# Every TensorE operand on a multiple of 512 bytes: padded and reordered buffers in a one-core decoder layer

## The chip, the cores and the metric

One core of a Trainium2 chip runs the whole kernel. The metric is device microseconds, from three runs. TensorE is called PE in the profile (PEld is its weight load), VectorE DVE, ScalarE ACT, GpSimd POOL and SyncE SP. On-chip memory has 128 partitions; an address here is the byte within a partition.

## The reference

One layer of a decoder over 512 tokens and 1024 channels, float32. The heart of it is matmuls: an input projection of 1024 to 8968 columns that feeds four token mixers (sliding-window attention A, a conformer convolution B, forgetting attention C, block-sparse attention D) and their gates; a projection of each branch back to 1024; the output projection; and a gated feed-forward part of 1024 to 5632 and 2816 to 1024.

```python
h = rmsnorm(x, ln1_g)
z = h @ w_in
(qa, ka, va, ub, qc, kc, vc, fc, qd, kd, vd, gz) = jnp.split(z, IN_SPLITS, axis=-1)
gates = jax.nn.sigmoid(gz.reshape(bsz, seq, N_BRANCH, D_MODEL) + b_gate)
ya = sliding_window_gqa(qa, ka, va, sinks, rel_bias[:, :SWA_HEADS])
yb = conformer_conv(ub, conv_w, conv_b, conv_ln_g, conv_ln_b)
yc = forgetting_attention(qc, kc, vc, fc, b_fgate)
yd = moba_attention(qd, kd, vd, rel_bias[:, SWA_HEADS:])
branches = jnp.stack([ya, yb, yc, yd], axis=2)
proj = jnp.einsum('bsnc,ncd->bsnd', branches, w_br)
merged = jnp.einsum('bsnd,bsnd->bsd', gates, proj)
x = x + merged @ w_out
h2 = rmsnorm(x, ln2_g)
u = causal_depthwise_conv(h2 @ w_up, ffn_conv_w, ffn_conv_b)
g_ff, v_ff = jnp.split(u, 2, axis=-1)
x = x + (jax.nn.silu(g_ff) * v_ff) @ w_down
return rmsnorm(x, final_g)
```

## The kernel before

Each float32 operand is split into a high and a low part, both of type float32r, and a product is made of three matmuls: high by high, low by high, high by low. The activations of the first norm are `hh` and `hl`, `[128, 8, 512]` each: eight slices of 128 channels by 512 tokens, 2048 bytes a slice. Weights come from HBM into `raw` (two buffers), ACT copies a half of a slab into `whi`, DVE subtracts to get `wlo` (three buffers each, taken in turn), and PE reads both. A dense unit is one block of 128 output channels: for k = 0 to 7 a trio, `whi` by `hh`, `wlo` by `hh`, `whi` by `hl`, 24 matmuls of 512 columns, with the 128x128 weight tile as the stationary operand and a slice of `hh` or `hl` as the moving one (line 244, in `t_mm`). V projections (line 297) have it the other way round: slices of `hh` stationary, weights moving, 256 or 264 columns. So have the output projection (lines 971 and 1013: slices of `merged` stationary, weights moving) and the down projection (line 1122: slices of `ah` and `al` stationary). Attention (lines 454, 455, 482, 509 and their like for branch A) reads `stA`, `stD`, `stE`, `stG`, `P`, `PTh`, `PTl` and `v`. In the feed-forward part `hh` and `hl` are used again for the second norm's output; the down projection's resident weights `wdh`, `wdl` take the same place afterwards.

Order is written out: a list of units, each followed by pieces of attention heads, evictions, splits and loads at fixed steps. Every tile comes from a pool with a stack on one side of the memory. `P0` (left, from the bottom) lives through the kernel; above it come `PI` (first norm), then `P1` (attention), then `PX` and `PW` (output projection). On the right side, from the top downwards, stand `PR` (one pad), `PY` (`acc` and the eight `y` buffers), later `PF` (`ah`, `al` and the feed-forward tiles). Tiles of a pool follow one another in the order of their first allocation; a ring of buffers takes the size of its largest tile, so `whi` and `wlo` take 4224 bytes, those of the first slab's `[128, 4, 264]` halves. Below `P0` lie 16384 bytes for the descriptors of GpSimd's transfers, then 128 bytes of constants.

GpSimd issues 18 transfers right after the first V units (lines 1336 to 1351: mask, bias rows, tables), later small ones of one row each for branch C (line 379). The bias rows in `rows` are transposed on PE at line 1361, `rb32` (the bias table) is a stationary operand at line 1374. The convolution's filters run on DVE between.

Of the kernel before, what the change touches and what calls it, by code (L numbers as in the profile page):

```python
# [8 lines left out]
F32 = mybir.dt.float32  # L9
R32 = mybir.dt.float32r  # L10
# [20 lines left out]
BR_A, BR_B, BR_C, BR_D = 0, 1, 2, 3  # L31
GL = 640
C_ID, C_TRI, C_MASK, C_N = 0, 128, 640, 1152


def f(ap):
    return ap.bitcast(F32)
# [16 lines left out]
def hybrid_layer_kernel(ctx: ExitStack, tc: tile.TileContext, x, ln1_g, w_in, b_gate, b_fgate, sinks,  # L54
                        conv_w, conv_b, conv_ln_g, conv_ln_b, w_br, w_out, ln2_g, w_up, ffn_conv_w,
                        ffn_conv_b, w_down, rel_bias, final_g, cst, onehot, gmask, out):
    nc = tc.nc
# [4 lines left out]
    def dap(t, off, ap):  # L62
        return bass.AP(tensor=t.tensor, offset=t.offset + off, ap=[list(a) for a in ap])

    def pool(name, side=None, space=None, bufs=1):
        kw = dict(name=name, bufs=bufs, reuse_waits="tile")
        if side:
            kw["side"] = side
        if space is not None:
            kw["space"] = space  # L70
        if space == DRAM:
            kw.pop("reuse_waits")
        return tc.alloc_tile_pool(**kw)

    P0 = pool("p0")
# [4 lines left out]
        return PD.tile([128, 512], F32, name="dps", tag="dps", bufs=3)  # L80


    ident = P0.tile([128, 128], F32, name="ident")
    hh = P0.tile([128, KD, S], R32, name="hh", tag="hh")
    hl = P0.tile([128, KD, S], R32, name="hl", tag="hl")
    pcA = P0.tile([128, 92], F32, name="pcA")
    pcB = P0.tile([128, 124], F32, name="pcB")
    pcC = P0.tile([128, 128], F32, name="pcC")
    nsk = P0.tile([128, 8], F32, name="nsk")
    sk = P0.tile([128, 8], F32, name="sk")  # L90
    bfg = P0.tile([128, 8], F32, name="bfg")
    P0.tile([128, 8], F32, name="pad")

    def col_gate(n, j):
        return pcA[:, n * 8 + j:n * 8 + j + 1]
# [45 lines left out]
        SP.dma_start(xs[t], dap(x, t * 128 * D, [[D, 128], [1, D]]))  # L141


    NRAW, NSP = 2, 3
    raws = []
    halves = []

# [13 lines left out]
    class Half:  # L161
# [10 lines left out]
        def split(self):  # L172
            src = self.raw.t[:, self.ks, self.cs]
            if self.dst is None:
                shape = [128, self.ks.stop - self.ks.start, self.cs.stop - self.cs.start]
                self.hi = P0.tile(shape, R32, name="whi", tag="whi", bufs=NSP)
                self.lo = P0.tile(shape, R32, name="wlo", tag="wlo", bufs=NSP)
            else:
                self.hi, self.lo = self.dst()
            yield ACT.activation(self.hi, src, AF.Copy)  # L180
            yield DVE.tensor_tensor(self.lo, src, f(self.hi), op=OP.subtract)  # L181
            self.raw.left -= 1
# [82 lines left out]


    PR = pool("pr", side="right")
    PR.tile([128, 8], F32, name="pad")
    PY = pool("py", side="right")
    acc = PY.tile([128, KD, S], F32, name="acc")  # L270

# [673 lines left out]
    def wo_load():  # L945
        PX = ctxP["px"] = pool("px")
        for t in range(NT):
            xt = PX.tile([128, D], F32, name="x1_%d" % t)
            SP.dma_start(xt, dap(x, t * 128 * D, [[D, 128], [1, D]]))
            x1.append(xt)  # L950
        PW = ctxP["pw"] = pool("pw")
        WO["h"] = PW.tile([128, KD, 512], R32, name="woh")
        WO["l"] = PW.tile([128, KD, 512], R32, name="wol")
        n2["g"] = PW.tile([128, D], F32, name="g2")
        SP.dma_start(n2["g"], dap(ln2_g, 0, [[0, 128], [1, D]]))
        n2["ss"] = PX.tile([128, 2, NT], F32, name="ss2")
        PX.tile([128, 8], F32, name="pad")

    oa = []

# [76 lines left out]
    def ffn_open():  # L1037

        PF = ctxP["pf"] = pool("pf", side="right")
        ffn["ah"] = PF.tile([128, NF, S], R32, name="ah")  # L1040
        ffn["al"] = PF.tile([128, NF, S], R32, name="al")
        n2["rb"] = PF.tile([128, S], F32, name="rb")
        ffn["fg"] = None

# [281 lines left out]
    PI.release()  # L1326
    PIP.release()
    P1 = ctxP["p1"] = pool("p1")
    rows = P1.tile([128, 3, 128], F32, name="rows", tag="P", bufs=2)
    em = P1.tile([32, 2 * GL], F32, name="em", tag="PTh", bufs=1)  # L1330
    gs = P1.tile([16, GL], F32, name="gs", tag="PTl", bufs=1)
    rb32 = P1.tile([32, 16], F32, name="rb32")
    Gd = PDR.tile([16, GL], F32, name="Gd")
    Gw = PDR.tile([128, 16, GL], F32, name="Gw")
    tm = ctxP["p1"].tile([128, 1024], F32, name="tm", tag="va", bufs=1)
# [61 lines left out]
    for u in units:  # L1397
# [4 lines left out]
        if u.adv:  # L1402
            step += 1
            if step == REL:
                ctxP["p1"].release()
                ctxP["ps1"].release()
                ctxP["w"] = pool("ps2", space=PSUM)
                wo_load()
            ps_ = head_pieces(step) + pieces.get(step, [])
# [12 lines left out]
        if u.idx == UP0:  # L1422
            u.out = u.mm(n2_last, 2)
            PY.release()
            ctxP["pw"].release()
            ffn_open()
            n2_rstd_dve()
        elif u.idx == UP0 + 1:
            u.out = u.mm(n2_rstd_pe, 4)
        elif u.idx >= NT:  # L1430
            u.out = u.mm()
# [73 lines left out]
```

## Time and profile before

| | |
|---|---|
| median of 3 runs | 1012.38 us (1012.28 to 1012.4) |
| profiled execution | 1012.8 us, its span 1011.0 us |
| instructions | 12462, of which 4840 matmuls |
| granted TensorE clock | 0.999 |
| HBM read, written | 99.10 MB, 7.51 MB |

The span is the time from the first to the last instruction that the trace shows; the execution's own time holds what lies around it. A row of a timeline has the start, the duration, the engine, the line, the operation, and the tiles as out<-in. Matmuls are pipelined: a duration of about 400 ns is the way of one matmul through the array, and the next one starts well before it ends. The distance from start to start is the rate at which PE goes on.

### The profile page before, as it was taken

Reading aid. Unit: us, or ns where it says so; the run is one execution under the profiler, and the core shown is the slowest. Engines: PE = TensorE matmul, PEld = TensorE weight load, DVE = VectorE, ACT = ScalarE, POOL = GpSimd, SP = SyncE. Lnnn points to the kernel's source line nnn. Section 1 sums busy time; section 2 is a strip of 40 time slices with the busy share of each in tenths; the row PEclk is TensorE's granted clock in tenths of the full one; section 3 lists DMA queues with packets and bytes.
Section 4 is the critical chain, followed back from the end, with each engine's and each line's share of the span. In section 5 each row is a group of like instructions: output and inputs, shape, how many; then the busy total and the mean of one; then the engine's idle time right before and its main releaser. Section 6 shows DMA issues by size and latency. Waiting matters only on the chain.

```text
span 1011.0 us, 12462 instructions
## 1 busy us (share of the span) xinstructions
PE 999.1 (99%) x4840; PEld 826.8 (82%) x4840; DVE 666.9 (66%) x1188; ACT 448.4 (44%) x782; POOL 23.2 (2%) x49
## 2 busy tenths in 40 slices
PE   8999999999999999999999999999999999999997
PEld 6888887989888888888888888888888888888886
DVE  6557777777878688896665445677767677733404
ACT  5435455455455545557424233443444444432302
POOL 1300000000000000000000000000000000000000
PEclk9999999999999999999999999999999999999999
DMA  7435532132233133232136430232233223334102
GB/s 251 105 112 186 164 85 85 42 105 81 67 107 122 43 84 100 66 97 93 42 125 208 146 125 1 84 125 84 83 100 109 84 84 110 120 124 146 63 1 84
DMA packets 101099, 102.18 MB, mean 101 GB/s; under 512 B 3377, under 2 KB 88544, under 8 KB 101040
## 3 DMA queue, kind: packets, MB, share of 16 engines
q1 hardware_dynamic: 99264, 99.31, 31.0%
q0 software_dynamic: 1200, 1.03, 0.4%
q10 hardware_dynamic: 576, 1.05, 0.3%
q8 instruction: 38, 0.62, 0.3%
q14 instruction: 21, 0.17, 0.1%
HBM read 99.10 MB, written 7.51 MB: 105 GB/s over the span
## 4 chain that ended last, share of the span: by engine, by line
PE 92%; DVE 4%; ACT 2%; issue 1%; DMA 1%; SPq 0%; DVEq 0%; ACTq 0%
PE dps L244 63%; PE wps L1122 8%; PE dps L1122 5%; PE dps L297 4%; PE dps L1013 2%; PE wps L971 2%; PE tps L482 2%; PE yps L509 1%; PE sps L455 1%; PE sps L454 1%; ACT P L437 1%; DMA raw<-in_w_in_dram 1%; PE yps L627 1%; DVE stE L386 1%; DVE P L475 1%
## 5 line engine op out<-in xcount | busy, mean ns | idle before, releaser
L244 PE MATMUL dps<-hh,whi 128*128 128x512 f32 x848 | 337.5, 398 | 0.0
L244 PE MATMUL dps<-hh,wlo 128*128 128x512 f32 x848 | 336.0, 396 | 0.0
L244 PE MATMUL dps<-hl,whi 128*128 128x512 f32 x848 | 332.0, 392 | 0.0
L181 DVE TENSOR_TENSOR wlo<-raw,whi 128x1024 fp32r<-128x1024 f32 (+1 forms) x152 | 185.5, 1222 | 95.2 <-ACT whi L180 95.0
L180 ACT ACTIVATE whi<-raw 128x1024 fp32r<-128x1024 f32 (+1 forms) x152 | 159.6, 1054 | 97.9 <-PE wps L1122 37.9
L244 PEld LDWEIGHTS dps<-hl,whi 128*128 128x128 f32 x848 | 161.2, 190 | 37.5
L244 PEld LDWEIGHTS dps<-hh,whi 128*128 128x128 f32 x848 | 159.5, 188 | 35.7 <-ACT v L307 0.2
L244 PEld LDWEIGHTS dps<-hh,wlo 128*128 128x128 f32 x848 | 159.4, 188 | 33.4
L437 ACT ACTIVATE P<-P,nm 128x128 f32<-128x128 f32 (+2 forms) x96 | 50.9, 531 | 76.9 <-DVE nm L435 76.3
L244 PE MATMUL dps<-y,whi 128*128 128x512 f32 x256 | 83.8, 399 | 0.0
L710 DVE SCALAR_TENSOR_TENSOR co<-hc,pcB,co 128x489 f32<-128x489 f32 (+25 forms) x120 | 82.5, 730 | 0.4
L1086 DVE SCALAR_TENSOR_TENSOR uy<-u,pcC,uy 128x511 f32<-128x511 f32 x88 | 65.8, 747 | 1.5
L244 PEld LDWEIGHTS dps<-y,whi 128*128 128x128 f32 x256 | 48.2, 188 | 10.9
L1078 DVE TENSOR_TENSOR u<-dps,rb 128x512 f32<-128x512 f32 x44 | 30.2, 687 | 36.8 <-PE dps L244 34.1
L244 PE MATMUL dps<-y,wlo 128*128 128x512 f32 x128 | 50.4, 394 | 0.0
L495 ACT ACTIVATE PTh<-tps 128x512 fp32r<-128x512 f32 (+1 forms) x48 | 24.4, 525 | 42.3 <-PE tps L482 41.9
L1122 PE MATMUL wps<-wlo,ah 128*128 128x512 f32 (+1 forms) x116 | 42.7, 368 | 0.0
L1122 PE MATMUL wps<-whi,ah 128*128 128x512 f32 (+1 forms) x116 | 42.7, 368 | 0.0
L1122 PE MATMUL wps<-whi,al 128*128 128x512 f32 (+1 forms) x116 | 42.7, 368 | 0.0
L1100 ACT ACTIVATE ah<-uy 128x512 fp32r<-128x512 f32 x22 | 13.9, 632 | 60.3 <-DVE uy L1099 60.3
L539 ACT ACTIVATE ytmp<-yps 64x512 f32<-64x512 f32 x24 | 14.3, 594 | 48.1 <-PE yps L509 24.9
L1092 ACT ACTIVATE uy<-uy 128x512 f32<-128x512 f32 x22 | 13.9, 632 | 43.6 <-DVE uy L1086 43.6
(250 smaller groups left out, 1292.7 us busy)
## 6 DMA issues: line engine op xcount, KB each, us to landing
raw<-in_w_up_dram SPq DMA_DIRECT2D x22, 1024.0 KB, 5.1
raw<-in_w_in_dram SPq DMA_DIRECT2D x40, 512.0 KB, 3.9
raw<-in_w_in_dram SPq DMA_DIRECT2D x14, 1024.0 KB, 5.2
raw<-in_w_down_dram SPq DMA_DIRECT2D x10, 1024.0 KB, 5.1
raw<-in_w_br_dram SPq DMA_DIRECT2D x16, 512.0 KB, 3.5
Gw<-Gd SPq DMA_DIRECT2D x8, 640.0 KB, 7.0
x<-in_x_dram SPq DMA_DIRECT2D x8, 512.0 KB, 8.5
raw<-in_w_out_dram SPq DMA_DIRECT2D x4, 1024.0 KB, 5.1
```

Of the source, the lines that this page charges most:

```text
L180: yield ACT.activation(self.hi, src, AF.Copy)
L181: yield DVE.tensor_tensor(self.lo, src, f(self.hi), op=OP.subtract)
L244: PE.matmul(ps, lhsT=a, rhs=b, start=n == 0, stop=n == 3 * nk - 1)
L297: PE.matmul(ps[:, :n], lhsT=l, rhs=r[:, k % 4, :], start=not done, stop=len(done) == 3 * KD - 1)
L437: ACT.activation(P[:, sl], P[:, sl], AF.Exp, bias=nm[:, i:i + 1], scale=-1.0, accum_out=sm[:, i:i + 1])
L482: PE.transpose(ps[:, c:c + 128], o["P"][:, PO[qb] + kb * 128:PO[qb] + kb * 128 + 128], ident)
L495: ACT.activation(o["PT"][0][:, sl], ps[:, :c], AF.Copy)
L710: DVE.scalar_tensor_tensor(co[c][:, d:], hc[:, :S - d], col_cw(CW - 1 - d, c), co[c][:, d:], op0=OP.mult, op1=OP.add)
L971: PE.matmul(oa[t], lhsT=l, rhs=r, start=k == 0 and i == 0, stop=k == KD - 1 and i == 2)
L1078: DVE.tensor_tensor(u, ps, n2["rb"], op=OP.mult)
L1086: DVE.scalar_tensor_tensor(y[:, d:], u[:, :S - d], col_fw(2 - d, j), y[:, d:], op0=OP.mult, op1=OP.add)
L1122: PE.matmul(ps, lhsT=l, rhs=r, start=k == first_k and i == 0, stop=k == last_k and i == 2)
```

## The change

No instruction is added, removed or put elsewhere; only the places of tiles differ.

- A tile `lead` of 384 bytes comes first in `P0`, and the area for GpSimd's descriptors shrinks from 16384 to 8192 bytes.
- The rings `whi` and `wlo` are allocated right behind `hh` and `hl`, each buffer 1152 floats (4608 bytes); a half takes the first part of it.
- The pads at the ends of `P0`, `PR`, `PX` grow, and `PF` gets one behind `al`.
- `rb32` is no tile of its own but a fourth slice of `rows`.

```diff
+LEAD, PADS, WPAD = 96, (136, 120, 88, 56), 1152
...
+    lead = P0.tile([128, LEAD], F32, name="lead")
     ident = P0.tile([128, 128], F32, name="ident")
     hh = P0.tile([128, KD, S], R32, name="hh", tag="hh")
     hl = P0.tile([128, KD, S], R32, name="hl", tag="hl")
+    NRAW, NSP = 2, 3
+    for n in ("whi", "wlo"):
+        for _ in range(NSP):
+            P0.tile([128, WPAD], R32, name=n, tag=n, bufs=NSP)
...
-    P0.tile([128, 8], F32, name="pad")
+    P0.tile([128, PADS[0]], F32, name="pad")
...
-                self.hi = P0.tile(shape, R32, name="whi", tag="whi", bufs=NSP)
-                self.lo = P0.tile(shape, R32, name="wlo", tag="wlo", bufs=NSP)
+                self.hi, self.lo = (P0.tile([128, WPAD], R32, name=n, tag=n, bufs=NSP)[:, :shape[1] * shape[2]].rearrange(
+                    "p (k c) -> p k c", k=shape[1]) for n in ("whi", "wlo"))
...
-    PR.tile([128, 8], F32, name="pad")
+    PR.tile([128, PADS[1]], F32, name="pad")
...
-        PX.tile([128, 8], F32, name="pad")
+        PX.tile([128, PADS[2]], F32, name="pad")
...
         ffn["al"] = PF.tile([128, NF, S], R32, name="al")
+        PF.tile([128, PADS[3]], F32, name="pad")
...
-    rows = P1.tile([128, 3, 128], F32, name="rows", tag="P", bufs=2)
+    rows = P1.tile([128, 4, 128], F32, name="rows", tag="P", bufs=2)
...
-    rb32 = P1.tile([32, 16], F32, name="rb32")
+    rb32 = rows[:32, 3, :16]
...
-    nc = bacc.Bacc("TRN2", target_bir_lowering=False, num_devices=1)
+    nc = bacc.Bacc("TRN2", target_bir_lowering=False, num_devices=1, dynamic_dma_scratch_size=8192)
```

## Rows read from the trace of the kernel before

**Rows 1.** The page, part 1: busy us, share of the span, instructions.
```profile
PE 999.1 (99%) x4840; PEld 826.8 (82%) x4840; DVE 666.9 (66%) x1188; ACT 448.4 (44%) x782; POOL 23.2 (2%) x49
```

**Rows 2.** The page, part 4: the chain that ended last, by engine.
```profile
PE 92%; DVE 4%; ACT 2%; issue 1%; DMA 1%; SPq 0%; DVEq 0%; ACTq 0%
```

**Rows 3.** Waits of PE: total us, times, longest us; first and last of five.
```profile
PE wz L1268 <- DVE eps L1263: 1.2, 1, 1.2
...
PE dps L297 <- ACT hh L131: 0.8, 1, 0.8
```

**Rows 4.** Busy us by stretch: PE, PEld, DVE, ACT, POOL, clock, DMA share, GB/s.
```profile
45.00:500.00 455.00, 452.70 (x2327) 381.70 (x2326) 346.97 (x719) 235.56 (x485) 12.71 (x26) 1.00 0.31 93
200.00:300.00 100.00, 99.87 (x527) 84.76 (x526) 80.77 (x159) 51.14 (x103) 2.60 (x5) 1.00 0.28 85
```

**Rows 5.** Timeline of PE in the up-projection: starts of units, and one trio.
```profile
691.73 0.40 PE L244 MATMUL dps<-hh,whi 128*128 128x512 f32 x1
...
697.28 0.40 PE L244 MATMUL dps<-hh,whi 128*128 128x512 f32 x1
...
697.75 0.40 PE L244 MATMUL dps<-hl,whi 128*128 128x512 f32 x1
697.99 0.40 PE L244 MATMUL dps<-hh,whi 128*128 128x512 f32 x1
698.23 0.39 PE L244 MATMUL dps<-hh,wlo 128*128 128x512 f32 x1
...
702.89 0.40 PE L244 MATMUL dps<-hh,whi 128*128 128x512 f32 x1
...
708.44 0.40 PE L244 MATMUL dps<-hh,whi 128*128 128x512 f32 x1
```

**Rows 6.** Line 244: durations, ns, min/median/max; first and last start.
```profile
L244 PE MATMUL dps<-hh,whi x848: 389/396/500, 26.7 to 880.4; 128*128 128x512 f32 x170
...
L244 PE MATMUL dps<-hh,wlo x848: 389/397/398, 27.0 to 880.7; 128*128 128x512 f32 x170
...
L244 PE MATMUL dps<-hl,whi x848: 388/389/404, 27.2 to 880.9; 128*128 128x512 f32 x170
```

**Rows 7.** Timeline of PE and its weight loads in the tail, 256 columns.
```profile
1002.75 0.28 PE L1122 MATMUL wps<-wdh,ah 128*128 128x256 f32 x1
...
1002.86 0.28 PE L1122 MATMUL wps<-wdl,ah 128*128 128x256 f32 x1
1002.87 0.19 PEld L1122 LDWEIGHTS wps<-wdh,al 128*128 128x128 f32 x1
...
1003.46 0.28 PE L1122 MATMUL wps<-wdh,ah 128*128 128x256 f32 x1
```

**Rows 8.** Groups of PE by form, count: 512 float32r columns, first and last.
```profile
L244 PE MATMUL dps<-hh,whi 128*128 128x512 f32 x848 | 337.5, 398 | 0.0
...
L455 PE MATMUL sps<-stE,stG 68*128 68x512 f32 x8 | 3.1, 393 | 0.0
```

**Rows 9.** Timeline of POOL: first and last of 18 issues, then the first stE.
```profile
22.18 0.68 POOL L1336 DMA_DIRECT2D tm<-in_cst_dram  x1 [21.72 <-PE tp L1296]
...
31.88 0.50 POOL L1351 DMA_DIRECT2D cY<-con  x1
44.66 1.00 POOL L379 DMA_DIRECT2D stE<-cY  x2 [12.28 <-DMA cY<-cn]
```

**Rows 10.** DMA issues: count, KB each, us from issue to landing.
```profile
rows<-in_ffn_conv_w_dram POOLq DMA_DIRECT2D x1, 64.0 KB, 2.6
```

**Rows 11.** Timeline of PE: who reads rows, and the first who reads stE.
```profile
46.03 0.46 PE L1361 MATMUL tps<-ident,rows 92*128 92x92 f32 x3
...
59.00 0.27 PE L455 MATMUL sps<-stE,stG 68*128 68x128 f32 x1
```

**Rows 12.** Line 1268, the bf16 warm-up: durations, ns.
```profile
L1268 PE MATMUL wz<-wz x19: 379/634/634, 1.2 to 8.9; 128*128 128x512 bf16 x19
```

**Rows 13.** Line 1122, the down projection's wlo: durations, ns.
```profile
L1122 PE MATMUL dps<-wlo,ah x42: 389/396/397, 943.0 to 980.9; 128*128 128x512 f32 x42
```

More of the change, by code (lines that the diff above doesn't have):

```diff
@@ L141, in x_load @@
         SP.dma_start(xs[t], dap(x, t * 128 * D, [[D, 128], [1, D]]))
-    NRAW, NSP = 2, 3
     raws = []
```

## The prediction, made before the result was known

> **What bounds the kernel now.** I read the busy shares first: PE 99% of a span of 1011.0 us, DVE 66%, ACT 44% [rows 1]. The chain that ended last is PE for 92% [rows 2], and the five largest waits of PE, 1.2 down to 0.8 us, add up to 5 us [rows 3]. So the time is the number of matmuls times the distance from one start to the next, and that distance is what an operand's address could change. [...] In the up-projection, where nothing but such matmuls runs, a unit is 24 of them (8 trios of hh·whi, hh·wlo, hl·whi). Four units begin at 691.73, 697.28, 702.89 and 708.44 us [rows 5]: they take 5.55, 5.61 and 5.55 us, which is 231, 234 and 231 ns a matmul. [...]
>
> [...] The three units have the same instructions and differ in which of the three whi and wlo buffers holds the weights. I added up the tile sizes in order of allocation (16384 bytes of descriptor area, 128 of constants, each tile rounded up to 32). Counted from a multiple of 512, hh and hl (the moving operands) and all their k-slices begin at byte 128; the whi buffers, 4224 bytes each, at 128, 256, 384; the wlo buffers at 0, 128, 256; ah and al at 160, y and merged at 448, woh and wol at 64, v and stA to stG at 448. The middle unit (whi at 256, wlo at 128) is the slow one. The durations by operand say more: hl with whi has a median of 389 ns, hh with whi 396, hh with wlo 397, though all stream 512 columns from byte 128 [rows 6]. A weight load starts about 0.01 us behind the start of a matmul [rows 7] and is for the next one. So during hl·whi the next slice of the same whi is loaded, during the other two a tile of another ring. hl·whi is the one case where the moving stream, the weights in use and the weights being loaded can share one remainder (whi at 128; at 384 they agree modulo 256). With a trio at 5.55/8 = 694 ns and one member 7 to 8 ns shorter, hl·whi comes to about 227 ns and the others to about 234. In the unit with whi at 256 a trio takes 5.61/8 = 701: no short member is left.
>
> So the trace shows two levels, near 227 and near 234, and the low one where the remainders agree. It also shows a third: at the second trio of the slow unit two distances are 0.24 us (697.75, 697.99, 698.23) [rows 5].
>
> **The change, part by part.** The lead tile (384 bytes) and the smaller descriptor area put ident at 8704 and hh at 9216, both multiples of 512; the six weight buffers become 4608 bytes (9 times 512) and stand right behind hl; the pads bring the tiles of P1, y and acc, woh and wol, ah and al to multiples of 512. No instruction is added, removed or moved on any engine or queue. What can change is the distance of matmuls.
>
> Matmuls of 512 float32r columns: 848 in each of the three groups of L244 with hh or hl, down to 8 in the smaller one of L455, 23 groups [rows 8], together 3646. Their mean distance, from the three units, is (5.55+5.61+5.55)/72 = 232.1 ns. With every remainder at zero each trio member is in the position of hl·whi: 227 ns. Sum: 3646 x 5.1 ns = 18.6 us. The ends: at best 17 ns less than 396 (the bf16 row, below), at worst the 0.24 us class. I take the low level because it is the row whose remainders are nearest to the new layout. Against it stands that it sits at byte 128 and not 0, which is why both ends stay in the picture.
>
> [...]
>
> Narrower matmuls: L297 and L1122 hold some 420 of 256 columns; six of them in the tail start over 0.71 us (1002.75 to 1003.46) [rows 7], 118 ns each, 50 us in all. The same 2.2% would be 1.1 us, the other end is 0; I take 0, since no row splits them into two classes. The first slab (264 columns, slices 1056 bytes apart), the hx tiles of the first transposes and the co tiles keep odd places; I count nothing for them, and nothing is lost there either.
>
> Descriptor area: POOL issues 18 transfers from 22.18 to 31.88 us, one in about 0.5 us [rows 9], while one takes some 2.6 us to land [rows 10]. So several are in the area at once. If half of it made each issue wait for the landing before, the rows would be complete 26 us after 22.18, at 48, where their reader, L1361, starts at 46.03, and the stE transfer now issued at 44.66 would wait until 69, where L455 starts at 59.00 [rows 11]: PE would stand up to 10 us. The other end is 0, and I take that: no issue waits now, and the cover is 14 us and more. rb32 inside rows makes L1361 wait for one landing more, over 15 us earlier, and holds that P buffer until L1374; the first head's P takes the other one.
>
> A PE 2% faster meets DVE at 81% in its fullest 100 us and a DMA share of 0.28 [rows 4]: neither is late next.
>
> The profiled execution took 1012.8 us, 1.8 more than its span; the median of three runs is 1012.38. 1011.0 - 18.6 is a span of 992.4, or 994.2 for that execution and 993.8 against the median. I say 994; the likeliest case spans 988 (the narrow ones too, every member at 226) to 1004 (half of the matmuls gain).
>
> **Rivals.** *Full rate.* [...] A bf16 matmul of 512 columns in the warm-up takes 379 ns at its shortest [rows 12], 17 less than the 396 of hh·whi. 3646 x 17 = 62 us, and half of it on the 420 narrower, 4: 946. For: no matmul of the kernel has both operands on a multiple of 512. Against: bf16 moves half the bytes; and wlo's first buffer, a third of its group in L1122, is on such a multiple as moving operand, yet no member of that group is shorter than 389 [rows 13]. [...]
>
> *Nothing.* The pattern could come from the order of the rings and not from places, or from bits far above 512: 1012, within 2 us. For: the group just named. Against: rows 5.
>
> *Slower.* Two streams that begin on equal places could meet at every step; the 0.24 us pairs would then be the rule. 3646 x (240-232) = 29 us: 1041. With 5 to win and 8 to lose on each, it decides from 39% of the matmuls on. For: such pairs exist, and which bits make them I can't tell, while every address moves by kilobytes. Against: where the remainders agree, hl·whi goes from 388 to 404 at most [rows 6].
>
> **How the numbers follow.** Forecast 0.47, full rate 0.20, nothing 0.14, slower 0.19 (a part of it mild, up to 1016, POOL's 10 us with it). A measurement here tells 0.2%, some 2 us, from no change. Faster holds the first two, 0.67; same 0.14; slower 0.19. The range reaches from the full rate, 944, to 1016: it leaves out the heavy part of the slower case and little more; 988 to 1004 is the likeliest one's own.
>
> **What would show it.** Right: three units of equal length in the up-projection, 5.45 us, and medians of hh·whi and hh·wlo down at the 389 of hl·whi. Full rate: units of 5.2 us, durations near 380. Nothing: 5.55 and 5.61 again. Slower: units of 5.7 us and durations over 400. Descriptors: pauses among POOL's issues, and PE idle before L1361 or L455. The prediction as a whole is wrong if matmuls with equal remainders are not equally far apart.

## Result, and the profile after

The changed kernel takes 998.37 us (median of 4 runs, 997.44 to 998.96), the kernel before 1012.39 (4 runs, 1012.28 to 1012.47): ratio 0.9861, 95% interval 0.9844 to 0.9878. The forecast was 994 with 988 to 1004 as its own range. The profiled execution took 997.44 us, its span is 995.6 us, 15.4 less than before.

Nothing moved between engines. The first parts of the page, busy times and the chain by engine, answer to [rows 1, 2]:

```profile
PE 982.3 (99%) x4840; PEld 824.9 (83%) x4840; DVE 666.9 (67%) x1188; ACT 450.3 (45%) x782; POOL 23.2 (2%) x49
...
PE 86%; DVE 7%; ACT 4%; issue 1%; DMA 1%; SPq 0%; DVEq 0%; ACTq 0%
```

PE has the same 4840 matmuls in 17 us less and is still 99% busy; DVE's work is the same to 0.1 us. So the gain is in the distance of matmuls. In the chain DVE and ACT now hold 11% where they held 6%. The timeline of the changed kernel's up-projection, one row in eight trios, answers to [rows 5]:

```profile
684.75 0.39 PE L250 MATMUL dps<-hh,whi 128*128 128x512 f32 x1
...
690.19 0.39 PE L250 MATMUL dps<-hh,whi 128*128 128x512 f32 x1
...
695.63 0.39 PE L250 MATMUL dps<-hh,whi 128*128 128x512 f32 x1
...
701.07 0.39 PE L250 MATMUL dps<-hh,whi 128*128 128x512 f32 x1
```

24 matmuls take 5.44 us each time, 226.7 ns apiece, where they took 5.55, 5.61 and 5.55. The durations of line 250 (min/median/max ns) answer to [rows 6]:

```profile
L250 PE MATMUL dps<-hh,whi x848: 387/389/496, 26.7 to 867.7; 128*128 128x512 f32 x170
...
L250 PE MATMUL dps<-hh,wlo x848: 386/389/402, 27.0 to 867.9; 128*128 128x512 f32 x170
...
L250 PE MATMUL dps<-hl,whi x848: 387/389/401, 27.2 to 868.1; 128*128 128x512 f32 x170
```

All three members of a trio are now at the 389 ns that hl·whi alone had. Over all matmuls of 512 float32r columns the mean distance from start to start, taken from the starts in the trace, 42 of 300 ns and more left out in either, fell from 232.2 to 227.4 ns.

### The profile page after: what moved, and what is told of

It is laid out like the page before. It is cut to its first block, busy times and chain, and to the rows that moved or that the text cites. A ratio compares the mean times of both kernels' runs of the same rounds, so it can differ in the third digit from the quotient of the medians.

```text
span 995.6 us, 12462 instructions
## 1 busy us (share of the span) xinstructions
PE 982.3 (99%) x4840; PEld 824.9 (83%) x4840; DVE 666.9 (67%) x1188; ACT 450.3 (45%) x782; POOL 23.2 (2%) x49
## 4 chain that ended last, share of the span: by engine, by line
PE 86%; DVE 7%; ACT 4%; issue 1%; DMA 1%; SPq 0%; DVEq 0%; ACTq 0%
PE dps L250 58%; PE wps L1129 8%; PE dps L1129 5%; PE dps L303 4%; PE dps L1019 2%; PE wps L977 2%; PE tps L488 2%; DVE wlo L187 1%; ACT P L443 1%; PE yps L515 1%; DVE P L481 1%; DVE stE L392 1%; PE sps L461 1%; PE sps L460 1%; ACT stD L391 1%
## 5 line engine op out<-in xcount | busy, mean ns | idle before, releaser
L250 PE MATMUL dps<-hh,whi 128*128 128x512 f32 x848 | 333.0, 393 | 0.0
L250 PE MATMUL dps<-hh,wlo 128*128 128x512 f32 x848 | 330.5, 390 | 0.0
L250 PEld LDWEIGHTS dps<-hl,whi 128*128 128x128 f32 x848 | 159.2, 188 | 33.6
```

The costliest lines, as they stand in the source:

```text
L250: PE.matmul(ps, lhsT=a, rhs=b, start=n == 0, stop=n == 3 * nk - 1)
```

## Experiments

Two theories were put against each other. *Agreement*: a matmul is quick when the moving operand, the weights in use and the weights being loaded share one remainder, wherever that lies. *Multiples*: an operand off a multiple of 512 costs on its own.

**All operands off by the same 128 bytes** (e1, the changed kernel; both sides of the memory are shifted).

```diff
-LEAD, PADS, WPAD = 96, (136, 120, 88, 56), 1152
+LEAD, PADS, WPAD = 128, (136, 216, 88, 56), 1152
```

> The changed kernel with every operand moved 128 bytes off the multiples of 512 (lead 512 bytes, the right side's pad 864): all remainders are 128, still equal. Agreement (what counts is that the moving operand, the weights in use and the weights being loaded share one remainder): nothing changes, 998 us, units of 5.45 us in the up-projection, medians of 389 to 390 ns for hh and hl. Multiples (what counts is that an operand begins on a multiple of 512 and so touches fewer lines): most of the gain is gone, 1008 to 1014 us, medians of 396.

Measured: 997.40 us, ratio to before 0.9853 (0.9839 to 0.9868). No operand of a dense matmul lies on a multiple of 512 and the whole gain is there (the quickest run of the changed kernel took 997.44 us). Its line 250:

```profile
L250 PE MATMUL dps<-hh,whi x848: 387/389/496, 26.6 to 867.6; 128*128 128x512 f32 x170
L250 PE MATMUL dps<-hh,wlo x848: 387/389/401, 26.8 to 867.8; 128*128 128x512 f32 x170
L250 PE MATMUL dps<-hl,whi x848: 387/389/400, 27.0 to 868.0; 128*128 128x512 f32 x170
```

Agreement holds, multiples fails.

**hh and hl alone at 128** (e2; `ident`, which lies below `hh`, and later `wdh` and `wdl` move with them).

```diff
-LEAD, PADS, WPAD = 96, (136, 120, 88, 56), 1152
+LEAD, PADS, WPAD = 128, (136, 120, 88, 56), 1152
...
+    P0.tile([128, 96], F32, name="gap")
     NRAW, NSP = 2, 3
```

> The changed kernel with hh and hl alone at remainder 128 (and wdh, wdl, which take their place), weights and all else at 0. Agreement: each of the 2544 matmuls with hh or hl loses its partner, 6 to 6.5 ns each, 16 us: 1013 to 1015 us, units of 5.6 us, all three medians at 396. Multiples: one of two operands is off, about half of it: 1004 to 1008 us.

Measured: 1010.19 us, ratio 0.9977 (0.9968 to 0.9987). Most of the gain is lost, though 3 us less than agreement had put and 2 us more than multiples had. The distance with hh and hl is 232.9 ns, 5.5 more than in the changed kernel, where 6 to 6.5 had been expected; the medians of line 251 are 393 ns and not 396.

```profile
L251 PE MATMUL dps<-hh,whi x848: 390/393/497, 26.6 to 880.0; 128*128 128x512 f32 x170
L251 PE MATMUL dps<-hh,wlo x848: 387/393/404, 26.8 to 880.3; 128*128 128x512 f32 x170
L251 PE MATMUL dps<-hl,whi x848: 388/393/404, 27.0 to 880.5; 128*128 128x512 f32 x170
```

**The wlo ring alone at 128** (e3), and at 256 (e5, with gaps of 64 and 64 floats in place of 32 and 96).

```diff
-    for n in ("whi", "wlo"):
+    for n, g in (("whi", 32), ("wlo", 96)):
         for _ in range(NSP):
             P0.tile([128, WPAD], R32, name=n, tag=n, bufs=NSP)
+        P0.tile([128, g], F32, name="gap" + n)
```

> The changed kernel with the wlo ring alone at remainder 128. Agreement: hl with whi keeps 389 ns, hh with whi (wlo is loaded beside it) and hh with wlo (wlo in use) go back to 396: 13 ns a trio, some 850 trios of L250 with hh, 128 with y, and 1 to 2 us in the down projection: 1010 to 1013 us, units of 5.55 us. Multiples: only the matmuls that use wlo pay, a third: 1002 to 1005 us, hh with whi stays at 389.

Measured: 1007.98 us, ratio 0.9955 (0.9940 to 0.9970), 2 us under what agreement had put, but the pattern of its medians is the one expected. Line 251 of e3:

```profile
L251 PE MATMUL dps<-hh,whi x848: 387/396/500, 26.5 to 877.5; 128*128 128x512 f32 x170
L251 PE MATMUL dps<-hh,wlo x848: 387/397/398, 26.7 to 877.7; 128*128 128x512 f32 x170
L251 PE MATMUL dps<-hl,whi x848: 388/389/398, 27.0 to 878.0; 128*128 128x512 f32 x170
```

These are the medians of [rows 6] again, 396, 397, 389. hh·whi uses no operand that was moved; what differs is the wlo tile that is loaded while it runs. With e2, where all weights agree with each other, the stream alone is off and the medians are 393, this says that the stream (393), the weights in use (hh·wlo, 397) and the weights on their way (hh·whi, 396) all have to agree for the 389 ns of the changed kernel.

> The changed kernel with the wlo ring alone at remainder 256. Agreement modulo 256: as the changed kernel, 998 us, all three medians of hh and hl at 389 to 390. Agreement modulo 512: as with the ring at 128, 1008 us, hh with whi and hh with wlo at 396 to 397.

Measured: 997.31 us, ratio 0.9853 (0.9837 to 0.9870). A difference of 256 bytes costs nothing that these runs show (the changed kernel took 997.44 us at its quickest); its hh·wlo:

```profile
L251 PE MATMUL dps<-hh,wlo x848: 387/389/401, 26.8 to 867.8; 128*128 128x512 f32 x170
```

That is 389 ns, where the same ring at 128 bytes had 397: what has to agree here is the remainder modulo 256, not modulo 512.

**The descriptor area alone** (e4, the kernel before).

```diff
-    nc = bacc.Bacc("TRN2", target_bir_lowering=False, num_devices=1)
+    nc = bacc.Bacc("TRN2", target_bir_lowering=False, num_devices=1, dynamic_dma_scratch_size=8192)
```

> The kernel before with the descriptor area alone halved: every tile on the left lies 8192 bytes lower, no remainder modulo 512 changes. Agreement: 1012.4 us, units of 5.55 and 5.61 us, medians 396, 397, 389. If the area itself or the high bits of the addresses made the gain: below 1010 us. If the smaller area held GpSimd up: pauses among its 18 issues after 22 us, which now come every 0.5 us.

Measured: 1012.41 us, ratio 0.9997 (0.9988 to 1.0007). Every tile on the left lies 8192 bytes lower, and nothing changes but the median of hl·whi, by 2 ns. Its line 244, and the last of the 18 transfers in its POOL timeline:

```profile
L244 PE MATMUL dps<-hh,whi x848: 389/396/500, 26.3 to 880.0; 128*128 128x512 f32 x170
...
L244 PE MATMUL dps<-hl,whi x848: 388/391/404, 26.8 to 880.4; 128*128 128x512 f32 x170
```

```profile
30.49 0.52 POOL L1351 DMA_DIRECT2D cY<-con  x1
31.00 0.50 POOL L1350 DMA_DIRECT2D cX<-con  x1
31.49 0.50 POOL L1351 DMA_DIRECT2D cY<-con  x1
```

GpSimd issues one every 0.5 us as in [rows 9]: half the area is enough here, and it is worth only the room.

**Equal remainders in the rings, and nothing else** (e6, the kernel before with the smaller area).

```diff
-                self.hi = P0.tile(shape, R32, name="whi", tag="whi", bufs=NSP)
-                self.lo = P0.tile(shape, R32, name="wlo", tag="wlo", bufs=NSP)
+                self.hi, self.lo = (P0.tile([128, 1088], R32, name=n, tag=n, bufs=NSP)[:, :shape[1] * shape[2]].rearrange(
+                    "p (k c) -> p k c", k=shape[1]) for n in ("whi", "wlo"))
```

> The kernel before with the descriptor area halved and the six weight buffers at 4352 bytes (17 times 256) instead of 4224, nothing else: hh, hl, whi and wlo then all have remainder 128 modulo 256, none lies on a multiple of 512, whi and wlo differ by 256 in part; y, ah, woh keep other remainders than their partners. Agreement modulo 256: the 2544 matmuls with hh or hl go from 232.0 to 227.3 ns, 12 us, less 1 us of waits: 1000 to 1003 us, units of 5.45 us. Agreement modulo 512 or multiples: at most a third of that, 1008 us or more.

Measured: 1002.21 us, ratio 0.9897 (0.9882 to 0.9912). 128 bytes more for each weight buffer bring 10 of the 15 us, with no tile at a multiple of 512. Its hh·wlo has what the changed kernel has:

```profile
L244 PE MATMUL dps<-hh,wlo x848: 387/389/397, 27.3 to 870.3; 128*128 128x512 f32 x170
```

**The distance by itself** (p1, p2). Behind the first V units, series of 48 matmuls on a tile of zeros, for instance

```diff
+    for i in range(48):
+        PE.matmul(wps[:, :512], lhsT=sw(0), rhs=mv(32), start=True, stop=True)
```

where `sw(o)` begins 4·o bytes and `mv(o)` 16384 + 4·o bytes into the tile, itself on a multiple of 512.

> The changed kernel with 18 series of 48 matmuls added behind the first V units; they read zeros of a tile of their own and write a bank that nobody reads. Moving m, stationary s, bytes from a multiple of 512. Agreement: 227 ns from start to start where m equals s (0/0, 128/128, 32/32, 256/256), 233 where they differ by 128, 64 or 32; a difference of 256 is as good as equal, or 1 ns worse; stationary in turn 0 and 128 gives 233 for both. Multiples: 227 at 0/0 alone, 233 or more wherever one operand is off, 128/128 and 32/32 the longest. Both: 256 columns are 119 ns at 0/0; bf16 215 to 216 ns.

The timeline of p1, merged by line: start, and time from the first start to the last end. A series of 11.04 us is (11.04 - 0.39)/47 = 227 ns from start to start, one of 11.35 us is 233.

```profile
26.56 11.04 PE L1343 MATMUL wz<-pt 128*128 128x512 f32 x48
37.44 11.35 PE L1345 MATMUL wz<-pt 128*128 128x512 f32 x48
48.63 11.36 PE L1347 MATMUL wz<-pt 128*128 128x512 f32 x48
59.82 11.06 PE L1349 MATMUL wz<-pt 128*128 128x512 f32 x48
70.72 11.05 PE L1351 MATMUL wz<-pt 128*128 128x512 f32 x48
...
92.49 11.37 PE L1355 MATMUL wz<-pt 128*128 128x512 f32 x48
103.69 11.08 PE L1357 MATMUL wz<-pt 128*128 128x512 f32 x48
114.61 11.15 PE L1359 MATMUL wz<-pt 128*128 128x512 f32 x48
...
136.50 11.36 PE L1363 MATMUL wz<-pt 128*128 128x512 f32 x48
147.70 11.04 PE L1365 MATMUL wz<-pt 128*128 128x512 f32 x48
...
169.74 11.08 PE L1369 MATMUL wz<-pt 128*128 128x512 f32 x48
180.66 11.35 PE L1371 MATMUL wz<-pt 128*128 128x512 f32 x48
191.85 5.90 PE L1373 MATMUL wz<-pt 128*128 128x256 f32 x48
197.59 5.86 PE L1375 MATMUL wz<-pt 128*128 128x256 f32 x48
203.30 10.53 PE L1377 MATMUL wz<-wz 128*128 128x512 bf16 x48
```

Moving and stationary at 0/0 (L1343), 128/128 (L1349) and 32/32 (L1357) are quick, and 256/0 (L1351) is; 128/0, 0/128 and 32/0 (L1345, L1347, L1355) are slow; weights in turn at 0 and 128 (L1363) are slow, at 0 and 256 (L1365) quick. With both operands walking through the tile, as in the kernel, the same two levels stand: equal (L1369) and 128 apart (L1371). A difference of 64 (L1359) was expected at 233 and is 229. bf16 has 215.8 ns. With 256 columns equal remainders are no gain: 119.9 ns against 118.6 at 128 bytes off (L1373, L1375). These three figures leave out the first six distances of a series.

> The changed kernel with 28 series of 48 matmuls added behind the first V units, on zeros, into a bank that nobody reads. Seventeen move the moving operand by 4 to 240 bytes against the stationary one: with agreement the shortest is 226.7 ns at a difference of 0, and every other lies between 227 and 234; if some other difference is shorter, equal remainders are not the best layout. Stationary and moving at the very same address: 227, if only the remainder counts; longer, if the two streams collide in a line. 64 stationary columns at equal remainders: 227 as before if the 11 ns over bf16 belong to the moving stream, nearer to 216 if they belong to the weight load; at 128 bytes off 230 instead of 233.4 if the excess goes with the length of the load. 256 columns off by 32 to 224: 116 to 120 ns, where 0 has 119.9. 384 columns: 170 at 0, 175 at 128.

Distances worked out from the starts of p2, in ns, without the first six of each series, for a moving operand that lies that many bytes behind the stationary one modulo 256:

```
512 columns:  4 236.7    8 233.3   16 231.8   32 233.4   48 233.3   64 228.9   80 231.0   96 233.4
            112 231.0  128 232.4  144 233.3  160 234.2  176 233.3  192 233.4  208 234.6  224 233.4  240 226.7
256 columns: 32 116.6   64 117.8   96 120.0  160 118.8  192 113.3  224 118.3      (0: 119.9, 128: 118.6)
384 columns:  0 173.3  128 176.0
```

Some of its series in the timeline:

```profile
205.46 11.05 PE L1375 MATMUL wz<-pt 128*128 128x512 f32 x48
216.34 11.08 PE L1377 MATMUL wz<-pt 128*128 128x512 f32 x48
227.26 11.20 PE L1379 MATMUL wz<-pt 128*64 128x512 f32 x48
238.30 11.26 PE L1381 MATMUL wz<-pt 128*64 128x512 f32 x48
...
272.10 5.61 PE L1391 MATMUL wz<-pt 128*128 128x256 f32 x48
```

No difference is quicker than 226.7 ns for 512 columns; 240 bytes (L1375) is as good as 0, which neither theory said. Both operands at the very same address (L1377) are as quick as far apart, 227 ns against p1's 227 at 0/0 (L1343), so reading the same bytes costs nothing extra here. With 64 stationary columns the distance is 230 (L1379), neither 216 nor 227: the 11 ns over bf16 do not fall with half as many stationary columns, and equal places lose 3 ns. At 128 bytes off it is 231 (L1381), so with 64 stationary columns the place makes 1 ns and not 6; why is open. For 256 columns the best of the eight differences measured is 192 (L1391), a place where 512 columns are slow.

**V halves at 192** (e7). The V units have 256 columns and weights that move; in p2 that length is quickest at 192 bytes (113.3 ns, 119.9 at 0), another place than the 0 of the other units' 512 columns (226.7 ns, 233.4 at 192). `v_slab` marks its halves, and `split` shifts them by 48 floats.

```diff
+                o = 48 if self.v else 0
                 self.hi, self.lo = (P0.tile([128, WPAD], R32, name=n, tag=n, bufs=NSP)[:, o:o + shape[1] * shape[2]].rearrange(
                     "p (k c) -> p k c", k=shape[1]) for n in ("whi", "wlo"))
...
+        for h in hs:
+            h.v = True
```

> The changed kernel with the whi and wlo halves of the V units put 192 bytes into their buffers; everything else as it is. In a V unit hh is stationary and the weights move, 256 columns; the probe has 113.3 ns for 256 columns at a difference of 192 bytes and 119.9 at 0. Agreement with a best difference that depends on the columns: the 288 matmuls of 256 columns in L305 or thereabouts go from 121 to about 115 ns, 1.9 us: 996 us against 997.5 to 998 of the changed kernel on the same chip, dense units unchanged at 5.45 us. If equal remainders are best for all lengths, or the probe's figure needs the very same operands over and over: no gain or a loss of 1 us.

> The changed kernel once more, to be set beside the one with shifted V halves on the same chip: 997 to 998.5 us, 256 columns of the V units at 121 ns.

Measured on one chip: 995.99 us with the shift (995.75 to 997.81), 997.87 for the changed kernel; ratios to before 0.9839 (0.9825 to 0.9852) and 0.9854 (0.9841 to 0.9868). The intervals overlap; the runs with a clock of 0.998 or 0.999 take 995.75 to 995.99 us with the shift and 997.02 and 997.25 without. What the gain rests on is the trace: the V units' matmuls in the changed kernel's second profile, and then with the shift.

```profile
L303 PE MATMUL dps<-whi,hh x128: 278/283/416, 9.8 to 240.1; 128*128 128x256 f32 x96, 128*128 128x264 f32 x32
L303 PE MATMUL dps<-wlo,hh x128: 280/283/415, 10.6 to 241.0; 128*128 128x256 f32 x96, 128*128 128x264 f32 x32
```

```profile
L308 PE MATMUL dps<-whi,hh x128: 276/276/392, 10.4 to 239.3; 128*128 128x256 f32 x96, 128*128 128x264 f32 x32
L308 PE MATMUL dps<-wlo,hh x128: 276/276/420, 11.2 to 240.2; 128*128 128x256 f32 x96, 128*128 128x264 f32 x32
```

283 became 276 ns, and the mean distance went from 119.9 to 113.8 ns (waits and the stretch at half clock, below, left out), the probe's figures. Over 288 matmuls that is 288 x 6 = 1.7 us; 1.9 had been expected. It is the quickest version measured.

## Why the prediction was right, step by step

- *The bound.* PE's distance sets the time: 17 us less of PE's busy time gave 15.4 us of span.
- *The mechanism.* hl·whi was read as the one case with equal remainders, and the other matmuls were put at its 227 ns. Units were to come to 5.45 us and are 5.44; the medians were to come to 389 and are. e1, e2, e3, e6 and the probe show that this is the cause. What the runs show is looser than the layout: modulo 256 (e5, 389 ns), and at every place that was measured (227 ns at 0/0, 128/128 and 32/32 in p1). The probe also shows where it ends: 240 bytes is as good as 0 (226.7 ns), and with 256 columns (119.9 ns, 113.3 at 192 bytes) or 64 stationary ones (230 ns, 231 at 128 bytes) equal places are not the quickest or hardly matter.
- *The sum.* 3646 x 5.1 = 18.6 us was forecast; 232.2 to 227.4 ns is 3646 x 4.8 = 17.3. The steady distance is 226.7, but one distance in eight still lies between 229 and 238. In the up-projection, where dense units follow one another, there is none; three quarters belong to line 250, nearly all of these in the first ten matmuls after PE comes back from other work and in the last two before it leaves. The probe has the same at its start: the first ten distances of L1357 have a mean of 229.8 ns, the last thirty 226.7. Why it takes that long is open.
- *Narrower matmuls.* Taken at 0 between 0 and a gain of 1.1 us; they lost 0.5 us over some 580 distances of 256 columns. For the V units that fits p1, 119.9 against 118.6 ns: their mean distance is 119.0 before and 119.9 after. So the step that put them at no loss was wrong by this half microsecond.
- *What is late next.* Here the prediction said nothing is, and that step was too light. The transposes of P on PE wait for DVE's normalisation (lines 475 and 481), those of lnn for a result of DVE too. What ended PE's idle time before the transposes of P (us, times), before, and then after:

```profile
  DVE P L475: 2.9, 9
...
  DVE PTl L501: 0.3, 1
```

```profile
  DVE P L481: 3.3, 10
...
  DVE PTl L507: 0.6, 2
```

The wait ahead of lnn (rows as in [rows 3]) before, and then after:

```profile
PE tps L756 <- DVE sm L587: 0.9, 1, 0.9
...
PE tps L762 <- DVE sm L593: 1.2, 1, 1.2
```

From start to start, with short waits that don't count as idle, the matmuls of 128 columns took 1.5 us more: 0.9 ahead of the transposes of P, 0.4 ahead of those of lnn. So 17.3 - 0.5 - 1.5 is the 15.3 to 15.4 us of the span.

- *The clock.* The other 1.4 us between 15.4 and the medians' 14.0 go with the clock. The profiled execution has a mean granted clock of 0.999, the other three 0.996 or 0.997, and they took 998.3 to 999.0 us instead of 997.4. Those three have no trace, but the second profile of the changed kernel (998.59 us, clock 0.996) shows a stretch at a lower clock. Its busy times by stretch (columns as in [rows 4]) and the row of PE's timeline ahead of it:

```profile
172.57 1.22 PE L488 MATMUL tps<-ident,P 128*128 128x128 f32 x4 [1.24 <-DVE P L481]
```

```profile
165.00:173.00 8.00, 6.76 (x33) 5.52 (x31) 4.64 (x12) 4.28 (x9) 1.44 (x3) 1.00 0.48 134
173.80:177.00 3.20, 3.20 (x17) 3.20 (x17) 2.26 (x4) 2.36 (x5) 0.00 (x0) 0.50 0.00 0
178.00:186.00 8.00, 8.00 (x70) 8.00 (x69) 5.15 (x12) 3.85 (x10) 0.00 (x0) 1.00 0.01 3
```

From 173.8 to 177.0 us the clock is at 0.50; 3.2 us at half pace would be 1.6 us lost, an estimate from that clock, and the span is 996.8 us where the first profile has 995.6. PE had stood for 1.24 us just before, waiting for DVE. e7's trace has the same: a wait of 1.24 us in front of the transposes of P, then the half clock from 174.7 to 178.1 us. The first profile, e1 and e5 have the same wait and no such stretch. The traces of the kernel before and of the changed one also end at the half clock (0.50 from 1009.9 and from 994.4 us on), once PE is done (busy 0.00 us there), which costs nothing; without the stretch in the middle the traces of these kernels read 0.998 or 0.999, with it 0.996 and 0.997. By that sign it came in 10 of the 25 runs of the five versions whose trace has a wait of 1.22 or 1.24 us there (the changed kernel, e1, e5, e6, e7), and in 1 of the 59 runs, with a clock on record, of the kernel before, e2, e3 and e4, whose traces have 1.08 to 1.15 us. That the wait has a part in it is likely and not shown, since the five are also the versions in which PE is quickest.

- *Descriptor area, rb32 in rows.* Taken at 0; e4 shows 0 for the area (ratio 0.9997). rb32 was not tried alone.
- *Rivals.* Full rate, which put the matmuls on multiples of 512 at the pace of bf16, failed: on multiples of 512 too, equal remainders give 226.7 ns for float32r, where bf16 has 215.8 in the probe, and no run shows a shorter steady distance for 512 float32r columns. Nothing and slower failed with the result and with e1 to e6; distances of 0.24 us became rarer, 66 before and 10 after. The weight load beside a matmul can cost it time: hh·whi takes 396 ns in e3, where only the loaded tile lies elsewhere, and 389 in the changed kernel.

## What to carry to other kernels

Where PE is 99% busy, compare the distance of matmul starts between units that differ in nothing but their buffers: a pattern with the period of a ring, here 5.55, 5.61, 5.55 us, points to addresses. For float32r matmuls of 512 columns with 128 stationary ones, give moving and stationary operands equal addresses modulo 256 and size ring buffers in multiples of 256 bytes (226.7 ns in the probe, 228.9 to 236.7 at differences of 4 to 224 bytes); absolute alignment was not needed (e1, 997.40 us), and 256 columns want another difference, here 192 bytes (113.3 ns, 119.9 at 0). Then look at what a quicker PE meets next: here the wait at one transpose grew with it, from 1.08 to 1.24 us, and in the runs at the lower clock 1 to 2 us more were lost.

## What the runs showed of the hardware that was not expected

- A float32r matmul of 512 columns came to no less than 226.7 ns in a steady series, against 215.8 for bf16; half as many stationary columns do not lower it (230). What the 11 ns are stays open.
- The best of the differences measured depends on the length: 0 or 240 bytes for 512 columns (226.7), 192 for 256 (113.3, half of 226.7). Why is open.
- A difference of 4 bytes is the slowest series measured, 236.7 ns.
- With 64 stationary columns equal places (230 ns) and 128 bytes off (231) are nearly the same.
